# Attention by pairs of heads: 64-row logit products on both halves of the rows

## The chip, the cores and the metric

One core of one Trainium2 chip. The metric is the device time of one execution in microseconds (us). TensorE (PE) does the matrix products, VectorE (DVE), ScalarE (ACT) and GpSimd (POOL) the work on vectors, SyncE (SP) issues the transfers.

## The reference

Two layers over 1024 new frames and 32 further frames of a stream with a cache of 512, width 1024. Layer 0 mixes tokens by stick-breaking attention (16 heads of 64), layer 1 by differential attention (8 heads, each with two score maps of 64). Each mixer is followed by an output projection, a layer norm, a squared-ReLU MLP of width 4096 and another norm. Cut to what the change touches:

```python
def _stick_breaking_block(q, q_pos, k, v, k_pos):
    z = jnp.einsum('bqhd,bkhd->bhqk', q, k) * (SB_HEAD_DIM ** -0.5)
    mask = k_pos[None, :] < q_pos[:, None]
    log_keep = jnp.where(mask, jax.nn.log_sigmoid(-z), 0.0)
    after = lax.cumsum(log_keep, axis=3, reverse=True) - log_keep
    w = jnp.where(mask, jnp.exp(jax.nn.log_sigmoid(z) + after), 0.0)
    return jnp.einsum('bhqk,bkhd->bqhd', w, v)

def _diff_block(q, q_pos, k, v, k_pos, lam):
    s = jnp.einsum('bqhcd,bkhcd->bhcqk', q, k) * (DIFF_HEAD_DIM ** -0.5)
    mask = (k_pos[None, :] // CHUNK) <= (q_pos[:, None] // CHUNK)
    p = jax.nn.softmax(jnp.where(mask, s, NEG_INF), axis=-1)
    a = p[:, :, 0] - lam * p[:, :, 1]
    return jnp.einsum('bhqk,bkhe->bqhe', a, v)
```

## The kernel before

Everything is kept with features on the 128 rows and the 1056 tokens (1024 + 32, in reversed order) along the columns. A number is held as a high part and a low part in a 32-bit format, and a product is three products: high x high, high x low, low x high (lines 299 to 301, the projections and the MLP, which are most of PE's work).

A mixer (from line 981) runs two streams of work that are written into each other. One is the supply (line 1092): projection units of q, k and v, 24 tiles of 128 outputs, each over three groups of 384, 384 and 288 tokens, and after them the first seven eighths of the output projection for group 0. The other is the attention of the eight pairs of heads. `fill` (line 1154) lets as much supply run as the attention's paid columns say, so that projections stand between the steps of attention on PE. The tile scheduler then orders the instructions of each engine by what is ready and by which buffers are free.

Attention of one head goes by pairs of query blocks (128 queries each). `scores` (line 684) makes a tile of logits of up to 512 keys for one block: a block `i` takes the keys from `i` to 7, cut at 4, so that a head has 12 tiles, 6 of 512 columns and 2 each of 384, 256 and 128. q's tile holds the high part of one head in 64 rows and its low part in the other 64; k's tile holds the high part twice, and `kl` the low part over zeros:

```python
        nc.tensor.matmul(z, q[:, qs], k[:, ks], start=True, stop=False)
        nc.tensor.matmul(z, q[:, qs], kl[:, ks], start=False, stop=b0 > i)
        if b0 == i:
            nc.tensor.matmul(z[:, 0:P], self.identb, mask, start=False, stop=True)
```

So two products over all 128 rows give the three partial products of one head, and a bf16 product adds the mask on the diagonal block. In layer 0 `stick` (715) then takes two sigmoids on ACT (725, 726), a running product on DVE (727) and a product (730); in layer 1 `softmax` (858) takes a maximum (863) and an exponential (869). `flip` (733) turns the weights around on PE (745), and ACT and DVE take them out of the bank as high and low parts (748, 146). `apply` (752) multiplies them with the values (761). `head_in` (640) makes the q and k tiles out of a projection: ACT lines 654 and 655, DVE lines 656 and 657, POOL's subtraction at line 146. The 32 further frames have small products of their own (lines 704, 708, 772, 774, 837, 838, 949, 950).

The eight banks of PSUM are dealt out as three for logits (`pz`), two for transposes and small sums (`pt`), one for outputs (`px`) and two for projections (`pd`).

Of the kernel before, what the change touches and what calls it, by code (L numbers as in the profile page):

```python
# [12 lines left out]
F32 = mybir.dt.float32  # L13
# [20 lines left out]
LEADS, LEADD = 0, 24  # L34
# [8 lines left out]
AHEAD = 2, 2  # L43
# [25 lines left out]
class Trunk:  # L69
# [5 lines left out]
    def __init__(self, ctx, tc, a):  # L75
# [5 lines left out]
        self.pz = ctx.enter_context(tc.tile_pool(name="pz", bufs=3, space=PSUM))  # L81
        self.pt = ctx.enter_context(tc.tile_pool(name="pt", bufs=2, space=PSUM))
# [175 lines left out]
    @staticmethod  # L258
    def qkv_order(kind):

        if kind == "diff":
            return [t for p in range(NP) for t in (2 * p, 2 * p + 1, 2 * NP + p)]
        order = [0, 2 * NP]
        for p in range(NP):
            order += [2 * p + 1] + ([2 * NP + p + 1, 2 * p + 2] if p + 1 < NP else [])
        return order
# [120 lines left out]
    def norm_last(self, pool, y, idx, g, s, x=None, dest=None):  # L387
# [28 lines left out]
        ps = self.pt.tile([P, 2, NQ], F32, name="pc", tag="pt")  # L416
# [61 lines left out]
    def token_means(self, t, n):  # L478
# [3 lines left out]
        ps = self.pt.tile([P, NQ], F32, name="pc", tag="pt")  # L482
# [9 lines left out]
    def spread(self, r, n, exact=False):  # L492
# [4 lines left out]
        if exact:  # L497
# [3 lines left out]
            ps = self.pt.tile([P, 512], F32, name="pr", tag="pt")[:, :n]  # L501
# [6 lines left out]
        ps = self.pt.tile([P, 512], F32, name="pr", tag="pt")[:, :n]  # L508
# [131 lines left out]
    def head_in(self, kind, h, g, raw, dst):  # L640
# [4 lines left out]
        if kind == "diff":  # L645
# [14 lines left out]
        if g == NG - 1:  # L660
            j = h % 2
            js = slice(j * HD, (j + 1) * HD)
            nc.vector.tensor_scalar(qd[js, j * DEC:(j + 1) * DEC], raw[qs, n - DEC:], SCALE, None, op0=ALU.mult)
            nc.vector.tensor_copy(kd[js], raw[ks, n - DEC:])
# [19 lines left out]
    def scores(self, qk, i, b0, b1, mask):  # L684

        nc = self.nc
        q, k, kl = qk
# [27 lines left out]
    def stick(self, z, n, rows, carry):  # L715
# [17 lines left out]
    def flip(self, pair, i2, b):  # L733
# [4 lines left out]
        ps = self.pt.tile([P, 4, P], F32, name="pt", tag="pt")  # L738
# [13 lines left out]
    def apply(self, po, wt, i2, b, prods):  # L752

        order = (b + 1, b) if b == i2 else (b, b + 1)
        for kb in order:
            for e, (v, s) in enumerate(prods(kb)):
                r = wt[:, s, kb - b]
                o = po
                if kb == i2:
                    r, o = r[:, P:], po[:, :P]  # L760
                self.nc.tensor.matmul(o, v, r, start=kb == i2 + 1 and b == i2 and e == 0,  # L761
                                      stop=b == NQ - 2 and kb == order[1] and e == len(prods(kb)) - 1)
# [218 lines left out]
    def mixer(self, kind, x, res, xpool, side, grow):  # L981
# [199 lines left out]
        for m in range(ahead):  # L1181
            for f in prepare(m):
                f()
# [211 lines left out]
```

## Time and profile before

| | |
|---|---|
| Median of 3 runs | 2953.78 us (2953.05 to 2954.75) |
| Profiled execution, its own time | 2956.23 us |
| Its span from the first to the last instruction | 2954.2 us |
| PE / DVE / ACT / POOL busy | 2823.1 / 1851.4 / 1244.9 / 1055.4 us |
| Attention of layer 0, with the projections in it | about 18 to 606 us |
| Attention of layer 1, with the projections in it | about 1480 to 2070 us |

A busy PE includes the tail of each product, which runs under the next one; the distance from one start to the next tells what a product takes out of PE's time. Between the two attention stages lie the output projection, the norms and the MLP.

### The profile page before, as it was taken

The page shows a single profiled execution, that of the slowest core. Times are in us where ns is not written, and L with a number is a line of the kernel's source. Part 1 is how long each engine was busy: PE and PEld are TensorE (multiplying, and loading weights), DVE is VectorE, ACT ScalarE, POOL GpSimd, SP SyncE. Part 2 cuts the span into 40 slices and gives each one's busy share as a digit, 9 for nine tenths or more (in the row PEclk, how much of TensorE's full clock was granted, in tenths as well). Part 3 has the DMA queues.
Part 4 walks back from the last instruction along what each step waited for, and adds up shares of the span by engine and source line. Part 5 has one row for each costly group of instructions (what it writes and reads, how often), then busy time and mean ns, then how long its engine had stood idle before and what let it go on. Part 6 is the DMA issues. An engine that isn't in the chain of part 4 may idle for free.

```text
span 2954.2 us, 46333 instructions
## 1 busy us (share of the span) xinstructions
PE 2823.1 (96%) x17640; PEld 2703.3 (92%) x17640; DVE 1851.4 (63%) x3491; ACT 1244.9 (42%) x2715; POOL 1055.4 (36%) x840
## 2 busy tenths in 40 slices
PE   8999999898999999999889999998989999999997
PEld 7888888798999999999878888886989999999996
DVE  7999999969533323334878888888695333223347
ACT  6666666635222211222545555555352222212224
POOL 3222222455322222222665554554653222222233
PEclk9999999899999999999989999997999999999998
DMA  4111111252211111111421111112522111111113
GB/s 152 57 52 56 56 51 35 67 169 79 65 44 46 47 43 50 45 53 54 135 71 50 52 55 54 57 57 81 178 71 63 47 47 47 45 46 47 51 58 102
DMA packets 106622, 194.78 MB, mean 66 GB/s; under 512 B 12704, under 2 KB 30496, under 8 KB 106272
## 3 DMA queue, kind: packets, MB, share of 16 engines
q1 hardware_dynamic: 105680, 189.17, 20.8%
q8 instruction: 139, 2.28, 0.3%
q10 hardware_dynamic: 576, 1.57, 0.1%
q0 software_dynamic: 144, 1.08, 0.1%
q14 instruction: 83, 0.68, 0.1%
HBM read 159.33 MB, written 32.44 MB: 65 GB/s over the span
## 4 chain that ended last, share of the span: by engine, by line
PE 68%; DVE 22%; issue 3%; ACT 3%; POOL 2%; DMA 1%; SPq 0%; DVEq 0%; ACTq 0%; POOLq 0%
PE pd L299 20%; PE pd L300 20%; PE pd L301 20%; DVE keep L727 4%; PE po L761 2%; DVE wt L146 2%; DVE beta L730 2%; PE pt L745 2%; DVE nmax L863 1%; DVE q L657 1%; ACT e L869 1%; PE z L691 1%; DVE k L656 1%; PE z L692 1%; DVE vacc L373 1%
## 5 line engine op out<-in xcount | busy, mean ns | idle before, releaser
L299 PE MATMUL pd<-xh,w 128*128 128x384 f32 (+1 forms) x2688 | 888.1, 331 | 20.1 <-ACT xh L1233 6.3
L300 PE MATMUL pd<-xl,w 128*128 128x384 f32 (+1 forms) x2688 | 876.1, 326 | 2.4 <-DVE xl L472 1.5
L301 PE MATMUL pd<-xh,w 128*128 128x384 f32 (+1 forms) x2688 | 877.4, 327 | 0.0
L146 POOL TENSOR_TENSOR w<-wraw,w 128x512 fp32r<-128x512 f32 x306 | 419.2, 1378 | 596.7 <-ACT w L196 582.8
L299 PEld LDWEIGHTS pd<-xh,w 128*128 128x128 f32 x2688 | 510.6, 190 | 36.3 <-issue 8.9
L300 PEld LDWEIGHTS pd<-xl,w 128*128 128x128 f32 x2688 | 510.1, 190 | 9.4 <-DVE xl L472 2.6
L299 PE MATMUL pd<-h,w 128*128 128x384 f32 (+1 forms) x1536 | 501.0, 327 | 11.3 <-DVE y L588 9.7
L301 PEld LDWEIGHTS pd<-xh,w 128*128 128x128 f32 x2688 | 509.8, 190 | 1.2
L146 POOL TENSOR_TENSOR w<-arena,w 128x512 fp32r<-128x512 f32 x189 | 256.7, 1361 | 710.4 <-ACT w L196 705.2
L300 PE MATMUL pd<-h,w 128*128 128x384 f32 (+1 forms) x1536 | 501.1, 326 | 1.1 <-DVE h L146 1.1
L301 PE MATMUL pd<-h,w 128*128 128x384 f32 (+1 forms) x1536 | 499.2, 325 | 0.0
L588 DVE TENSOR_TENSOR y<-y,pd 128x384 f32<-128x384 f32 (+1 forms) x336 | 174.0, 519 | 383.6 <-PE pd L301 383.3
L574 DVE TENSOR_TENSOR arena<-arena 128x384 f32<-128x384 f32 (+1 forms) x192 | 163.6, 853 | 357.5 <-ACT arena L573 357.2
L196 ACT CAST w<-wraw 128x512 fp32r<-128x512 f32 x307 | 189.1, 619 | 409.2 <-PE pd L300 343.6
L299 PEld LDWEIGHTS pd<-h,w 128*128 128x128 f32 x1536 | 292.6, 191 | 13.4 <-issue 6.0
L300 PEld LDWEIGHTS pd<-h,w 128*128 128x128 f32 x1536 | 293.3, 191 | 2.0 <-DVE h L146 1.4
L301 PEld LDWEIGHTS pd<-h,w 128*128 128x128 f32 x1536 | 292.9, 191 | 0.1
L196 ACT CAST w<-arena 128x512 fp32r<-128x512 f32 x189 | 116.7, 620 | 356.0 <-PE pd L300 330.2
L727 DVE TENSOR_TENSOR_SCAN keep<-keep,cols 128x512 f32<-128x512 f32 (+2 forms) x208 | 220.6, 1071 | 6.4 <-ACT keep L725 4.8
L761 PE MATMUL po<-wt,vt 128*128 128x256 f32 (+1 forms) x1120 | 193.7, 296 | 6.7 <-DVE ot L346 3.9
L573 ACT ACTIVATE arena<-pd 128x384 f32<-128x384 f32 (+1 forms) x192 | 88.7, 462 | 248.2 <-PE pd L301 240.0
L146 POOL TENSOR_TENSOR kl<-arena,k 64x384 fp32r<-64x384 f32 (+1 forms) x96 | 99.0, 1032 | 226.7 <-ACT k L655 206.0
(216 smaller groups left out, 4462.7 us busy)
## 6 DMA issues: line engine op xcount, KB each, us to landing
arena<-down SPq DMA_DIRECT2D x90, 256.0 KB, 2.6
wraw<-up SPq DMA_DIRECT2D x72, 256.0 KB, 2.6
arena<-up SPq DMA_DIRECT2D x72, 256.0 KB, 2.6
wraw<-down SPq DMA_DIRECT2D x70, 256.0 KB, 2.6
wraw<-sb_o SPq DMA_DIRECT2D x48, 256.0 KB, 2.7
wraw<-diff_o SPq DMA_DIRECT2D x48, 256.0 KB, 2.7
wraw<-diff_qkv SPq DMA_DIRECT2D x45, 256.0 KB, 2.7
wraw<-sb_qkv SPq DMA_DIRECT2D x24, 256.0 KB, 3.1
```

The costliest lines, as they stand in the source:

```text
L146: eng.tensor_tensor(out, x, hi.bitcast(F32), op=ALU.subtract)
L196: nc.scalar.copy(w[:, 0], raw)
L299: self.nc.tensor.matmul(ps, wh, xh, start=first, stop=False)
L300: self.nc.tensor.matmul(ps, wh, xl, start=False, stop=False)
L301: self.nc.tensor.matmul(ps, wl, xh, start=False, stop=last)
L573: nc.scalar.activation(r, ps, AF.Relu)
L574: nc.vector.tensor_tensor(r, r, r, op=ALU.mult)
L588: nc.vector.tensor_tensor(yo, yo, ps, op=ALU.add)
L727: nc.vector.tensor_tensor_scan(keep[:rows, 1:1 + n], keep[:rows, 1:1 + n], self.zero[:rows].broadcast_to([rows, n]), keep[:rows, 0:1], op0 ...
L730: nc.vector.tensor_tensor(beta[:rows, :n], beta[:rows, :n], keep[:rows, :n], op=ALU.mult)
L745: nc.tensor.transpose(ps[:, e], w[:, (kb - wb) * P:(kb - wb + 1) * P], self.ident)
L761: self.nc.tensor.matmul(o, v, r, start=kb == i2 + 1 and b == i2 and e == 0, stop=b == NQ - 2 and kb == order[1] and e == len(prods(kb)) - 1)
```

## The change

The two heads of a pair are taken together. The projections of q and k come in tiles of 128 rows with head 0 in the upper and head 1 in the lower 64 rows (`heads`, the weights' layout), and `head_in` makes a high and a low tile of each (`qh`, `ql`, `kh`, `kl`) in one instruction for both heads. `scores` makes two tiles of logits at once, in two banks, with three products over 64 rows for each, written so that the heads alternate. The masks come after all six. Three banks for logits and two for transposes become five for both; output, weights and masks stay. In layer 0 a job is now a pair of query blocks of both heads, whose outputs share a bank; steps of preparation are dealt out one by one between the steps of `flip`; the supply leads by 24 steps in layer 0 too, and its order is q, k, v in both layers. The first column of ones of `stick` is set once in four tiles of their own.

```diff
-        self.pz = ctx.enter_context(tc.tile_pool(name="pz", bufs=3, space=PSUM))
-        self.pt = ctx.enter_context(tc.tile_pool(name="pt", bufs=2, space=PSUM))
+        self.pz = ctx.enter_context(tc.tile_pool(name="pz", bufs=5, space=PSUM))
...
-        q, k, kl, qs, ks, qd, kd = dst
-        nc.sync.dma_start(out=self.a["o_" + kind + "_k"][h, :, gs], in_=raw[ks])
-        nc.scalar.mul(q[qs, gs], raw[qs], SCALE)
-        nc.scalar.copy(k[ks, gs], raw[ks])
-        nc.vector.tensor_copy(k[qs, gs], raw[ks])
-        nc.vector.scalar_tensor_tensor(q[ks, gs], raw[qs], SCALE, q[qs, gs].bitcast(F32),
-                                       op0=ALU.mult, op1=ALU.subtract)
-        self.lo(kl[qs, gs], raw[ks], k[ks, gs], nc.gpsimd)
...
+        hi, lo, own = dst
+        if t % 2:
+            keys = self.a["o_" + kind + "_k"][t - 1:t + 1, :, gs]
+            nc.sync.dma_start(out=keys.rearrange("h d t -> (h d) t"), in_=raw)
+            nc.scalar.copy(hi[:, gs], raw)
+            self.lo(lo[:, gs], raw, hi[:, gs], nc.gpsimd)
+            if g == NG - 1:
+                nc.scalar.copy(own, raw[:, n - DEC:])
+        else:
+            nc.scalar.mul(hi[:, gs], raw, SCALE)
+            nc.vector.scalar_tensor_tensor(lo[:, gs], raw, SCALE, hi[:, gs].bitcast(F32),
+                                           op0=ALU.mult, op1=ALU.subtract)
...
     def scores(self, qk, i, b0, b1, mask):
...
-        z = self.pz.tile([P, 512], F32, name="z", tag="z")[:, :n]
-        nc.tensor.matmul(z, q[:, qs], k[:, ks], start=True, stop=False)
-        nc.tensor.matmul(z, q[:, qs], kl[:, ks], start=False, stop=b0 > i)
-        if b0 == i:
-            nc.tensor.matmul(z[:, 0:P], self.identb, mask, start=False, stop=True)
-        self.pay(self.price[0] * n)
-        return z
+        zs = [self.pz.tile([P, 512], F32, name="z", tag="z")[:, :n] for _ in range(2)]
+        for e, (q, k) in enumerate(((qh, kh), (ql, kh), (qh, kl))):
+            for j, z in enumerate(zs):
+                js = slice(j * HD, (j + 1) * HD)
+                nc.tensor.matmul(z, q[js, qs], k[js, ks], start=e == 0, stop=e == 2 and b0 > i)
+        for z in zs:
+            if b0 == i:
+                nc.tensor.matmul(z[:, 0:P], self.identb, mask, start=False, stop=True)
+            self.pay(self.price[0] * n)
+        return zs
...
-        keep = self.att.tile([P, 520], F32, name="keep", tag="keep", bufs=4)
-        beta = self.att.tile([P, 512], F32, name="beta", tag="beta", bufs=6)
         if carry is None:
-            nc.vector.memset(keep[:rows, 0:1], 1.0)
+            keep = self.whole_sticks[0]
+            self.whole_sticks.rotate(-1)
         else:
-            nc.vector.tensor_copy(keep[:rows, 0:1], carry)
+            keep = self.att.tile([P, 520], F32, name="keep", tag="keep", bufs=2)
+            nc.scalar.copy(keep[:rows, 0:1], carry)
+        beta = self.att.tile([P, 512], F32, name="beta", tag="beta", bufs=BETAS)
...
-        ps = self.pt.tile([P, 4, P], F32, name="pt", tag="pt")
+        ps = self.pz.tile([P, 4, P], F32, name="pt", tag="z")
...
-            e = self.att.tile([P, 512], F32, name="e", tag="e", bufs=8)[:rows, :z.shape[1]]
+            e = self.att.tile([P, 512], F32, name="e", tag="e", bufs=12)[:rows, :z.shape[1]]
...
-                es = [self.softmax([self.scores(st["qk"][2 * p + h], i, b0, b1, self.maskb[:, P:2 * P])
-                                    for b0, b1 in chunks], P, (s0, s1[:, 0:1])[h]) for h in range(2)]
+                zs = [self.scores(st["qk"][p], i, b0, b1, self.maskb[:, P:2 * P]) for b0, b1 in chunks]
+                es = [self.softmax([z[h] for z in zs], P, (s0, s1[:, 0:1])[h]) for h in range(2)]
...
-        nqk, nout, self.nwt = (4, 1, 3) if diff else (2, 3, 4)
-        ahead, lag, lead = AHEAD[diff], LAG[diff], LEADD if diff else LEADS
+        nout, self.nwt = (1, 3) if diff else (2, 4)
+        ahead, lag, lead = AHEAD[diff], LAG[diff], LEAD
...
-            nc.gpsimd.dma_start(out=self.rope, in_=self.a["rope"])
+            nc.sync.dma_start(out=self.rope, in_=self.a["rope"])
...
-                nc.gpsimd.memset(kl[ks].bitcast(F32), 0.0)
...
-            todo = prepare(n + ahead) if n + ahead < len(jobs) else []
+            more = len(jobs[n + 1][2]) if n + 1 < len(jobs) else 0
             for e, f in enumerate(fins):
...
+                prepare(goal + -(-more * (e + 1) // len(fins)))
                 wait.append((p, f()))
```

How it moves the instructions on PE, at two places. A name's number is that of its tile: `z_...` is a tile of logits, `q`, `k`, `kl` before and `qh`, `ql`, `kh`, `kl` after are the tiles of queries and keys, `pd` a projection, `po` the outputs, `pt` transposes.

PE at the start of layer 0's attention, before:

```order
L691 MATMUL z_438<-k_183,q_182 128x512
L691 MATMUL z_448<-k_183,q_182 128x512
L691 MATMUL z_458<-k_183,q_182 128x256
L692 MATMUL z_458<-kl_184,q_182 128x256
L694 LDWEIGHTS identb_139
L694 MATMUL z_458<-maskb_141,identb_139 128x128
L301 MATMUL pd_397<-xh_89,w_83 128x384
L299 MATMUL pd_397<-xh_89,w_83 128x384
L692 MATMUL z_438<-kl_184,q_182 128x512
L692 MATMUL z_448<-kl_184,q_182 128x512
```

The same place after:

```order
L693 MATMUL z_523<-kh_188,qh_184 128x384
L693 MATMUL z_524<-kh_188,qh_184 128x384
L693 MATMUL z_523<-kh_188,ql_185 128x384
L693 MATMUL z_524<-kh_188,ql_185 128x384
L693 MATMUL z_523<-kl_189,qh_184 128x384
L693 MATMUL z_524<-kl_189,qh_184 128x384
L696 LDWEIGHTS identb_136
L696 MATMUL z_523<-maskb_138,identb_136 128x128
L696 LDWEIGHTS identb_136
L696 MATMUL z_524<-maskb_138,identb_136 128x128
```

Two products for each tile of one head became six alternating ones for the tiles of two heads (523 and 524), and the two masks stand behind them.

PE in layer 1, at the third and fourth query block of a pair, before:

```order
L691 MATMUL z_18949<-k_17693,q_17692 128x256
L692 MATMUL z_18949<-kl_17694,q_17692 128x256
L694 LDWEIGHTS identb_139
L694 MATMUL z_18949<-maskb_141,identb_139 128x128
L691 MATMUL z_18965<-k_17343,q_17342 128x128
L692 MATMUL z_18965<-kl_17344,q_17342 128x128
L694 LDWEIGHTS identb_139
L694 MATMUL z_18965<-maskb_141,identb_139 128x128
L761 MATMUL po_18680<-wt_18911,vt_17936 128x256 x6
```

There after:

```order
L693 MATMUL z_19929<-kh_19112,qh_18758 128x512
L693 MATMUL z_19929<-kh_19112,ql_18759 128x512
L693 MATMUL z_19929<-kl_19113,qh_18758 128x512
L294 MATMUL pd_20049<-xh_7247,w_79 128x384
L693 MATMUL z_19930<-kh_19112,qh_18758 128x512
L693 MATMUL z_19930<-kh_19112,ql_18759 128x512
L693 MATMUL z_19930<-kl_19113,qh_18758 128x512
L295 MATMUL pd_20049<-xl_7248,w_79 128x384
```

Here the two heads' tiles (19929 and 19930) stand apart: three products of one head, a projection product, three of the other.

## Rows read from the trace of the kernel before

**Rows 1.** The page, busy us, share of the span, instructions, of PE.

```profile
PE 2823.1 (96%) x17640; PEld 2703.3 (92%) x17640; DVE 1851.4 (63%) x3491; ACT 1244.9 (42%) x2715; POOL 1055.4 (36%) x840
```

**Rows 2.** Stretches of the two attention stages: busy us and count by engine, clock, DMA.

```profile
core 0: us, PE busy (x) PEld busy (x) DVE busy (x) ACT busy (x) POOL busy (x), PEclk, DMA share, GB/s
18.00:606.00 588.00, 554.93 (x3705) 508.54 (x3704) 537.92 (x1036) 392.81 (x895) 162.33 (x127) 0.99 0.20 60
1480.00:2070.00 590.00, 543.16 (x3377) 484.24 (x3376) 493.03 (x1194) 332.81 (x860) 315.26 (x287) 0.95 0.20 60
```

**Rows 3.** Waits of PE in the two stages: us in total, times, longest.

```profile
PE pt L745 <- DVE wt L146: 11.2, 17, 2.4
PE pt L745 <- DVE keep L722: 7.6, 8, 1.2
PE z L691 <- DVE k L656: 7.3, 1, 7.3
...
PE z L691 <- ACT e L869: 13.3, 12, 2.4
```

**Rows 4.** Timeline of PE in layer 0: start, busy us, instruction.

```profile
299.93 0.39 PE L691 MATMUL z<-k,q 128*128 128x512 f32 x1
300.16 0.39 PE L692 MATMUL z<-kl,q 128*128 128x512 f32 x1
300.39 0.23 PE L694 MATMUL z<-maskb,identb 128*128 128x128 bf16 x1
300.43 0.42 PE L299 MATMUL pd<-xh,w 128*128 128x384 f32 x1
300.69 0.34 PE L300 MATMUL pd<-xl,w 128*128 128x384 f32 x1
...
301.04 0.34 PE L691 MATMUL z<-k,q 128*128 128x384 f32 x1
301.21 0.34 PE L692 MATMUL z<-kl,q 128*128 128x384 f32 x1
...
302.26 0.28 PE L691 MATMUL z<-k,q 128*128 128x256 f32 x1
302.38 0.28 PE L692 MATMUL z<-kl,q 128*128 128x256 f32 x1
...
303.60 0.22 PE L691 MATMUL z<-k,q 128*128 128x128 f32 x1
303.66 0.27 PE L692 MATMUL z<-kl,q 128*128 128x128 f32 x1
303.77 0.23 PE L694 MATMUL z<-maskb,identb 128*128 128x128 bf16 x1
```

**Rows 5.** Timeline of PE around products of 64 and 32 rows.

```profile
84.61 0.34 PE L301 MATMUL pd<-xh,w 128*128 128x384 f32 x1
84.87 0.23 PE L772 MATMUL pts<-ident,beta 64*32 64x64 f32 x1
...
1585.65 0.72 PE L949 MATMUL pos<-wts,cv 128*128 128x32 f32 x5
1586.21 0.48 PE L691 MATMUL z<-k,q 128*128 128x512 f32 x1
1586.53 0.40 PE L692 MATMUL z<-kl,q 128*128 128x512 f32 x1
...
1660.41 0.40 PE L950 MATMUL pos<-wts,vs 32*128 32x32 f32 x2
1660.75 0.44 PE L691 MATMUL z<-k,q 128*128 128x384 f32 x1
1661.03 0.33 PE L692 MATMUL z<-kl,q 128*128 128x384 f32 x1
```

**Rows 6.** Groups by line, DVE: count, busy us, mean ns, idle before.

```profile
L657 DVE SCALAR_TENSOR_TENSOR q<-arena,q 64x384 fp32r<-64x384 f32 (+1 forms) x96 | 67.4, 702 | 4.2 <-ACT q L654 1.2
...
L656 DVE CAST k<-arena 64x384 fp32r<-64x384 f32 (+1 forms) x96 | 51.7, 539 | 14.6 <-ACT arena L1052 11.9
...
L724 DVE COPY keep<-keep 128x1 f32<-128x1 f32 (+1 forms) x72 | 10.2, 142 | 0.0
```

More of the change, by code (lines that the diff above doesn't have):

```diff
@@ L259, in qkv_order @@
     def qkv_order(kind):
[L261 to L266, printed above, removed]
+        return [t for p in range(NP) for t in (2 * p, 2 * p + 1, 2 * NP + p)]
     def weave(self, budget, us):
@@ L760, in apply @@
                     r, o = r[:, P:], po[:, :P]
-                self.nc.tensor.matmul(o, v, r, start=kb == i2 + 1 and b == i2 and e == 0,
-                                      stop=b == NQ - 2 and kb == order[1] and e == len(prods(kb)) - 1)
+                self.nc.tensor.matmul(o, v, r, start=kb == i2 + 1 and b == i2 and e == 0 and not shared,
+                                      stop=b == NQ - 2 and kb == order[1] and e == len(prods(kb)) - 1,
+                                      skip_group_check=self.two)
                 self.pay(self.price[3])
@@ new lines, in sb_jobs, with prep, fin, later @@
+        for i2 in range(0, NQ, 2):
+            left, box = {}, []
+            for c0, c1 in (((i2, 4), (4, NQ)) if i2 < 4 else ((i2, NQ),)):
+                ws = {}
+                def prep(e, i2=i2, c0=c0, c1=c1, ws=ws, left=left):
+                    i = i2 + e
+                    b0 = max(c0, i)
+                    for j, z in enumerate(self.scores(st["qk"][p], i, b0, c1, self.maskb[:, 0:P])):
+                        w, left[i, j] = self.stick(z, (c1 - b0) * P, P, left.get((i, j)))
+                        ws[j, e] = (w, b0)
+                def fin(j, b, i2=i2, ws=ws, box=box):
+                    wt = self.flip([ws[j, 0], ws[j, 1]], i2, b)
+                    vt = st["val"][p][0]
+                    def later():
+                        if not box:
+                            box.append(self.px.tile([P, 512], F32, name="po", tag="po"))
+                        po = box[0]
+                        self.apply(po[:, j * 2 * P:(j + 1) * 2 * P], wt, i2, b, lambda kb: [
+                            (vt[:, kb, j].rearrange("p a b -> p (a b)"), s) for s in range(2)], j > 0)
+                        if b == NQ - 2 and j:
+                            t = self.att.tile([HD, 512], F32, name="vlo", tag="vlo")
+                            nc.scalar.copy(t, po[HD:P])
+                            qs = slice(i2 * P, (i2 + 2) * P)
+                            for h in range(2):
+                                hs = slice(h * 2 * P, (h + 1) * 2 * P)
+                                nc.vector.tensor_tensor(st["out"](p)[h * HD:(h + 1) * HD, qs], po[0:HD, hs],
+                                                        t[:, hs], op=ALU.add)
+                    return later
+                jobs.append((p, [lambda e=e, f=prep: f(e) for e in range(2)],
+                             [lambda j=j, b=b, f=fin: f(j, b) for j in range(2) for b in range(c0, c1, 2)]))
@@ L996, in mixer @@
         xs = self.of_groups(x)
[L997 removed]
+        st = {"qk": {}, "val": {}, "small": {}, "cache": {}, "made": {}}
         ot, spill = {}, {}
@@ L1064, in split_next @@
                 fetch["open"] = True
-                for tag in ("q", "q", "k", "k") if diff else ("kl",):
-                    backs.append(self.att.tile([P, T], F32, name="back", tag=tag, bufs=nqk if diff else 2))
+                for tag in ("qh", "ql", "kh", "kl"):
+                    backs.append(self.att.tile([P, T], F32, name="back", tag=tag, bufs=2))
             here = [k for k in ended if k not in spill and k not in whole]
@@ L1251, in run @@
                 grow()
+                self.whole_sticks = deque(self.att.tile([P, 520], F32, name="stick", tag=f"stick{i}")
+                                          for i in range(4))
+                for t in self.whole_sticks:
+                    nc.gpsimd.memset(t[:, 0:1], 1.0)
             opool, o = self.mixer(kind, x, res, xpool, sides[0], grow)
```

127 lines of the change are left out of this document (50 added, 77 removed).

## The prediction

> **What bounds the kernel now.** I read the busy table first: TensorE (PE) is busy 2823.1 us, 96% of the span [rows 1]. The table of stretches puts the change in its place: it touches the two attention stages, 18 to 606 us (stick-breaking, "sb") and 1480 to 2070 us (differential, "diff"). There PE is busy 554.9 of 588 us and 543.2 of 590 us, so 33.1 + 46.8 = 79.9 us are idle; DVE is busy 537.9 us (91%) in the first and 493.0 us (84%) in the second [rows 2]. Both stages are PE-bound, with DVE close behind in the first. So the sum below is made of PE time, and other engines count only through PE's idle time. The named waits of PE say which part of that is for whom: in sb nearly all for DVE (11.2, 7.6 and 7.3 us), in diff the longest for ACT's exponentials, which free the banks of the logits (13.3 us) [rows 3].
>
> **Part 1, the products of the logits.** On PE I read the distance from one start to the next, since the busy times overlap. Between the two products of one tile it is 0.23 us at 512 columns, 0.17 at 384, 0.12 at 256; at 128 it is 0.06 and then 0.11 [rows 4]. Before, each tile takes two 128-row products, and there are 384 tiles, 12 for each of 16 heads in two layers: by the loops 192 of 512 columns and 64 each of 384, 256 and 128. That is 192 x 0.46 + 64 x (0.35 + 0.24 + 0.17) = 137 us. After, a tile takes three 64-row products, 1152 in all. Two of them on different halves of the rows may run side by side; no row of before shows two such products next to each other. If all ran in pairs the three passes would take 576 / 2 x 0.23 + 96 x (0.17 + 0.12 + 0.11) = 105 us, 32 less than before, and that is what the change is worth at most. But the order of the changed kernel doesn't pair them all. By its tile numbers, 786 of the 1152 stand next to one of the other half; 107 runs, with 288 products and 98,944 of 442,368 columns, belong to one head alone, most of them in diff, where the second head's tile comes later (the second place shown in the order). Laid side by side where a neighbour of the other half exists and end to end elsewhere, with the distances above, they take 134 us; all end to end, 205 us. I take 134, since the halves share neither rows nor bank. **Term: -3 us** (ends -32 and +68).
> The Trainium skill ("TensorE: Matmul & The Clock Gate", Part 3, the table of measured speedups) gives 3.07 times for four 32-row tiles side by side, not 4. By that loss, an estimate of mine, two halves give 1.54 rather than 2, the paired part takes some 21 us more, and the sum below would be 2994. No row here shows it.
>
> **Part 2, the masks.** A mask product follows the tile's last product at its usual distance, the next product starts 0.04 us later, and that one then takes 0.26 rather than 0.17 us [rows 4]; so a mask costs 0.13 us, 256 of them 33 us. In the new order 94 of the 256 come directly after another mask, and such a one should cost the 0.06 us of any product of 128 columns: 94 x 0.07. **Term: -7 us** (ends -12 and 0).
>
> **Part 3, changes of the row count.** Now PE goes from 128-row products to 64-row ones and back around every run of logits: 253 runs in the new order, none before. Before, a few small products of 64 and 32 rows show what that costs [rows 5]. Into 64 rows: L301 to L772 takes 0.26 us where products of 384 columns follow each other at 0.17 [rows 4], so 0.09 more. A whole visit: the two 32-row L950 run from 1660.41 to 1660.75, 0.34 us where two L949 take 0.22 (five in 0.56 us before 1586.21), so 0.12 more, and the following L691 takes 0.28 instead of 0.17, 0.11 more. Together 0.09 + 0.12 + 0.11 = 0.32 us. But L691 behind an L949 without any change of rows also takes 0.32 instead of 0.23: 0.09 belongs to the change of type, which the new products don't have. That leaves 0.23 us a visit, and 253 x 0.23 = 58 us. 42 of the runs come directly from a mask, whose own 0.09 us is then paid anyway: -4. **Term: +54 us.** Ends: 0, if the chip prepares a 64-row product of the same type ahead as it does a 128-row one (no row shows that pair), and 253 x 0.32 = 81. A gain is excluded, as no product gets shorter by it. I take 0.23, since every row with such a change has it.
> The Trainium skill says the same of the cause ("TensorEngine Tiling (Array Packing)", Key Properties): a change of tiling mode drains the engine, a change of tile within a mode doesn't. By that rule the alternation within a run is free, and only the 253 visits are charged, as I do.
>
> **Part 4, the other engines.** head_in now works on whole 128-row tiles, once for two heads. DVE loses the copy of k (51.7 us), half of the 67.4 us for the low part of q, and small copies and memsets that go to ACT and POOL, the carry copy of 10.2 us among them [rows 6]: 51.7 + 33.7 + 10.2, some 100 us over both stages. POOL loses its memsets of the low half of k and half of the subtractions that make it. None of this is on PE's path but where PE waits for it. In sb the waits for L656 and L722 (7.3 and 7.6 us) lose their instruction, and those for DVE's subtraction behind the transposes (11.2) may halve, since DVE's load falls from 91% to some 83%: 20 us. What is late next there is the scan L727 itself, which stays. In diff I take 5 us. **Term: -25 us** (ends -50, a little over half of the 79.9 idle, and +35, the third rival).
>
> **Part 5, costed at nothing.** Attention starts one more projection tile later in sb (q, k and v of the pair must be there) and the projections lead by 24 steps: 24 x 3 x 0.17 = 12 us of products are made earlier, none is added. The partial sums of the output projection cover the end of the stage; if they don't, PE's idle time there grows by up to those 12. One more spilled tile in sb and the rotary table's load on SP's queue instead of POOL's lie under a DMA share of 0.20 [rows 2]; SP's queue then holds the weights behind one more load, once. The column of ones and the carry copies move to ACT, which is busy 392.8 of 588 us.
>
> **Sum.** -3 - 7 + 54 - 25 = +19 us. The profiled execution took 2956.23 us for a span of 2954.2; the median of the timed runs is 2953.78, and the terms are added to that: 2953.8 + 19 = **2973 us**. With the ends of the drains and idle time that this case can still have, its own range is 2948 to 3015.
>
> **The rivals.**
> *No charge for the row change.* Weights of 64-row products are loaded ahead, so entries and exits are free; the place is every one of the 253 runs. For it: all small products in [rows 5] differ from the new ones in type or width too. Against: all of them pay, in and out. Then 2954 - 3 - 7 - 25 = 2919 us, faster than before. It decides at a charge of (3 + 7 + 25) / 253 = 0.14 us a visit: below that the change wins.
> *No overlap of the halves.* The two heads' products run one after the other: 205 instead of 134 us, 2973 + 71 = 3044 us. For it: nothing in the trace shows an overlap. Against: the halves have rows, weights and banks of their own.
> *The banks become the wait.* Logits, transposes and small sums now share five banks in turn, and diff takes four at once for a block with two pieces; a transpose behind them waits until exponentials free the oldest. It happens already for 12 tiles, 1.1 us each [rows 3]. If each of the 32 such blocks paid that once, +35 us, and DVE's relief of 5 us in diff is gone: 2973 + 40 = 3013 us. Against: PE's order has projections in between.
>
> **How the numbers follow.** Forecast 0.50 (of it 0.10 within 0.2%), no charge 0.22 (0.20 faster, 0.02 within), no overlap 0.15, banks 0.13. A measurement of this kernel can tell 0.2%, some 6 us, from no change. So faster 0.20, same 0.12, slower 0.68. The range goes from 2919 to 3035: it holds the forecast, most of the first rival and the third, and leaves out the second.
>
> **What would show it.** Step 1: in the profile after, products L693 of two heads that start within a few hundredths of a us of each other, and 0.23 us per pair at 512 columns; starts 0.23 apart for each alone mean no overlap. Step 3: the first L693 after a projection product starts 0.26 rather than 0.17 us behind it, and the mask or product behind a run comes late by 0.1. Step 4: PE's idle time in the two stages down to some 55 us, DVE's busy time there down by some 100. I am wrong if the first L693 follows at 0.17, or if the two stages together end more than 10 us earlier than their 1178 us.

## The result, and the profile after

The changed kernel takes 2985.8 us in the median (2983.8 to 2986.3), the kernel before 2953.7 us beside it on the same chip: a ratio of 1.0107 with a 95% interval of 1.0090 to 1.0125. It is 32 us slower; 19 us were forecast. The sum was near, but two of its terms were not, and one cost that decides the sign is not in it at all: that the total came so near is luck.

The busy line of the page after, to be read against [rows 1]:

```profile
PE 2871.4 (96%) x18024; PEld 2700.9 (90%) x18024; DVE 1712.7 (57%) x3091; ACT 1212.3 (41%) x2739; POOL 968.8 (32%) x779
```

PE is busy 48 us longer, DVE 139 us less. The table of stretches says where; columns as in [rows 2]. These are the two attention stages and the two ends of the output projections behind them (from the last product of an attention to the last of its output projection):

```profile
33.00:626.00 593.00, 577.59 (x3886) 501.11 (x3885) 489.97 (x748) 377.30 (x936) 134.10 (x95) 0.99 0.17 59
626.00:707.00 81.00, 71.57 (x445) 70.39 (x445) 59.15 (x77) 32.51 (x52) 46.49 (x34) 0.94 0.43 139
1514.00:2081.00 567.00, 558.99 (x3528) 476.91 (x3527) 405.92 (x1052) 303.41 (x818) 260.29 (x247) 0.96 0.18 60
2081.00:2187.00 106.00, 96.16 (x575) 93.95 (x574) 71.60 (x100) 41.07 (x67) 64.18 (x47) 0.94 0.44 143
```

In attention PE now idles 15 and 8 us, where it had 33 and 38. The ends of the output projections, 72 and 92 us long before, are 81 and 106 us, and PE idles 9 and 10 us there.

To compare kernels I split each span in three. *Idle* is the time in which PE does nothing. *Clock* is what the granted clock took: for each microsecond of the trace PE's busy time times (1 - clock), added up. The rest is *work*, PE's time at its full 2.4 GHz. All in us; attention is from the first logits to the last output product, both layers; idle elsewhere includes some 6 us at the start and 8 at the end. The last two columns are the median time and its ratio to the kernel before.

| kernel | span | work | idle in attention | idle elsewhere | clock | time | ratio |
|---|---|---|---|---|---|---|---|
| before | 2954.2 | 2771.4 | 70.4 | 60.5 | 51.9 | 2953.7 | |
| after | 2984.5 | 2817.4 | 23.0 | 89.6 | 54.5 | 2985.8 | 1.0107 |
| e_norm | 2940.8 | 2823.3 | 21.8 | 62.2 | 33.5 | 2944.5 | 0.9971 |
| b_share | 2955.3 | 2768.7 | 70.6 | 63.3 | 52.7 | 2957.6 | 1.0008 |
| e_2full | 2930.0 | 2751.5 | 40.0 | 86.6 | 51.9 | 2932.8 | 0.9931 |
| e_3full | 2981.7 | 2816.2 | 33.3 | 88.0 | 44.2 | 2981.1 | 1.0094 |
| e_mid | 2996.2 | 2858.7 | 18.9 | 62.7 | 55.9 | 2997.1 | 1.0140 |
| e_noalt | 2974.6 | 2809.7 | 24.2 | 91.1 | 49.6 | 2974.0 | 1.0068 |
| e_pair01 | 2952.7 | 2801.6 | 35.4 | 65.5 | 50.2 | 2948.1 | 0.9980 |
| e_dve | 2950.3 | 2821.7 | 25.8 | 63.5 | 39.3 | 2956.4 | 1.0005 |
| e_2full4 | 2951.7 | 2760.1 | 52.2 | 89.6 | 49.8 | 2956.8 | 1.0014 |
| e_2fulldve | 2952.8 | 2756.0 | 55.4 | 91.1 | 50.3 | 2964.3 | 1.0030 |
| e_mixed | 2947.5 | 2795.1 | 48.5 | 64.8 | 39.1 | 2949.4 | 0.9986 |
| e_mixsb | 2983.3 | 2789.8 | 63.0 | 64.9 | 65.6 | 2985.1 | 1.0098 |

Each row but the time is one execution. The three kernels with the same two full products (e_2full, e_2full4, e_2fulldve) differ by 9 us in work, and some spans lie up to 12 us off their median. So differences of up to 9 us in work carry nothing, nor do those of up to some 5 us in the other columns.

From before to after: work +46, idle in attention -47, idle elsewhere +29, clock +3; together +30 of span. The prediction had +44, -25, 0, 0.

### The profile page after: what moved, and what is told of

Same layout as the page of the kernel before. It is cut to its first block, busy times and chain, and to the rows that moved or that the text cites. A ratio compares the mean times of both kernels' runs of the same rounds, so it can differ in the third digit from the quotient of the medians.

```text
span 2984.5 us, 46210 instructions
## 1 busy us (share of the span) xinstructions
PE 2871.4 (96%) x18024; PEld 2700.9 (90%) x18024; DVE 1712.7 (57%) x3091; ACT 1212.3 (41%) x2739; POOL 968.8 (32%) x779
## 4 chain that ended last, share of the span: by engine, by line
PE 81%; DVE 14%; ACT 2%; issue 1%; POOL 1%; DMA 0%; ACTq 0%; DVEq 0%; POOLq 0%
PE pd L294 23%; PE pd L295 22%; PE pd L296 22%; PE z L693 4%; PE po L765 4%; PE pt L748 2%; DVE keep L730 2%; DVE beta L733 1%; DVE stick L730 1%; ACT e L876 1%; DVE vacc L368 1%; DVE nmax L870 1%; DVE wt L146 1%; DVE xl L467 1%; PE z L696 1%
## 5 line engine op out<-in xcount | busy, mean ns | idle before, releaser
L765 PE MATMUL po<-wt,vt 128*128 128x256 f32 (+1 forms) x1120 | 182.5, 292 | 7.3 <-DVE ot L823 4.8
L765 PEld LDWEIGHTS po<-wt,vt 128*128 128x128 f32 x1120 | 156.3, 195 | 20.4 <-issue 7.8
L146 DVE TENSOR_TENSOR wt<-pt,wt 128x384 fp32r<-128x384 f32 (+1 forms) x240 | 149.5, 628 | 40.0 <-ACT wt L751 37.4
```

The source lines that it names most:

```text
L146: eng.tensor_tensor(out, x, hi.bitcast(F32), op=ALU.subtract)
```

## The experiments

### Where the time outside attention came from

The change moves the transposes' two banks into the ring of the logits. The normalizations' small tiles (`pc`, means of tokens, and `pr`, a row spread over the partitions) lay in those two banks, and they moved along, also outside attention, where the output projection and the MLP use the ring. e_norm gives them two banks of their own there:

```diff
+    def small_bank(self, shape, name):
+        pool, tag = (self.pd, "pd") if self.banks[0][0] is self.pz else (self.pz, "z")
+        return pool.tile(shape, F32, name=name, tag=tag)
...
-        ps = self.pz.tile([P, NQ], F32, name="pc", tag="z")
+        ps = self.small_bank([P, NQ], "pc")
```

(and so for the other three; the products outside attention keep the ring of five for themselves). b_share tries the reverse on the kernel before: products outside attention go round all five banks, two of them the normalizations':

```diff
-[(self.pz, "z")]
+[(self.pz, "z")] * 3 + [(self.pt, "pt")] * 2
```

> The changed kernel with one part of it undone: outside the attention stages the small tiles of a normalization (means of tokens, and the row spread over the partitions) lie in two banks of their own again (those that feed the projections' products during attention), not in the ring of five that the output projection and the MLP use for their products. Theory A, the shared ring makes TensorE wait at the normalizations' small products: its idle time outside the attention stages falls from 83 us towards the 54 us of the kernel before, and the time from 2986 to 2957 to 2972. Rival B, those waits come from the new order of the work (what is left of the output projection, the state of the weights' loads), not from the banks: 2980 to 2990.

> The kernel before with one thing of the change alone: outside the attention stages the products of the output projection and the MLP go round five banks, of which two are those of the normalizations' small tiles, as in the changed kernel (before: three banks of their own, and two for the normalizations). Attention is untouched. Theory A, it is this sharing that costs: TensorE's idle time outside attention grows by 15 to 30 us and its clock falls there too, 2970 to 2995 us. Rival B, sharing costs only with the changed kernel's other order: 2948 to 2960.

e_norm takes 2944.5 us (2942.6 to 2946.7), 0.9971 of before, interval 0.9959 to 0.9983: 41 us less than the changed kernel, more than theory A gave, and faster than before. The waits of PE over the whole span (us in total, times, longest) show what the ring did. After:

```profile
PE pc L482 <- DVE vacc L370: 41.5, 6, 7.9
PE pr L509 <- DVE diag L506: 11.8, 7, 2.7
```

The same two in e_norm, four lines further down in the file:

```profile
PE pr L513 <- DVE diag L510: 8.0, 7, 3.9
PE pc L486 <- DVE vacc L374: 7.3, 5, 2.6
```

The second of them before:

```profile
PE pc L487 <- DVE vacc L375: 9.6, 5, 2.7
```

41.5 us of waiting for the sum of squares fell to 7.3. All idle time ahead of a `pc` outside attention, whatever ended it, is 11 us before, 47 after and 22 in e_norm, so not all of it is won back. The timeline (start, busy us, instruction, and in brackets the idle time ahead) shows one of the six, in the output projection of layer 0. After:

```profile
677.09 0.29 PE L296 MATMUL pd<-oh,w 128*128 128x288 f32 x1
677.22 0.81 PE L358 MATMUL pm<-acc,onesr 128*128 128x384 f32 x2
684.80 0.37 PE L482 MATMUL pc<-onesr,vacc 128*128 128x1 f32 x1 [6.77 <-DVE vacc L370]
```

e_norm:

```profile
677.28 0.81 PE L362 MATMUL pm<-acc,onesr 128*128 128x384 f32 x2
677.63 0.59 PE L296 MATMUL pd<-oh,w 128*128 128x288 f32 x1
...
685.73 0.29 PE L295 MATMUL pd<-ol,w 128*128 128x288 f32 x1
685.87 0.50 PE L486 MATMUL pc<-onesr,vacc 128*128 128x1 f32 x4
```

Between `pm` (the mean goes out to DVE) and `pc` (the squares come back) DVE needs some 8 us. In e_norm 60 projection products fill them. In the changed kernel none stand there: `pc` comes next in PE's order, and PE waits 6.77 us. All six waits are of this kind: at these places, three in each layer, the changed kernel has 0, 33 and 63 projection products between `pm` and `pc`; e_norm, as the kernel before, has 60 at the first, 87 at the second and 101 or more at the third. So the loss is one of order: with the tiles in one ring the scheduler put the small product ahead of projections. Why it did so, no run shows.

b_share takes 2957.6 us, 1.0008 (0.9999 to 1.0017): no cost, rival B. There the ends of the output projections get longer by 6 and 7 us, but the MLP's first product comes only 2 and 3 us later, and idle time outside attention grows by 3 us in all. At the three places it has 60, 87 and over 120 products ahead of `pc`, as before. So products in the normalizations' banks don't hurt by themselves; what hurts is the place that `pc` got in the changed kernel. Of e_norm's gain 29 us is idle time and 21 us clock, against 6 us more work. 12 of the 21 are in the differential stage, where the edit leaves all tiles where they were; why the clock is better there I did not settle (last section).

### What a row change costs

Three kernels with other products. e_2full and e_3full make two or three 128-row products of each tile (no row change, no overlap), with sums that mix the heads:

```diff
+        for z in zs:
+            for e, (q, k) in enumerate(((qh, kh), (ql, kh), (qh, kl))[:2]):
+                nc.tensor.matmul(z, q[:, qs], k[:, ks], start=e == 0, stop=e == 1 and b0 > i)
```

e_mid, on e_norm, adds visits: the masks go behind the first two of the six products.

```diff
+            if e == 0 and b0 == i:
+                for z in zs:
+                    nc.tensor.matmul(z[:, 0:P], self.identb, mask, start=False, stop=False)
         for z in zs:
-            if b0 == i:
-                nc.tensor.matmul(z[:, 0:P], self.identb, mask, start=False, stop=True)
```

> The changed kernel with two 128-row products for each tile of logits in place of three 64-row ones (it sums the rows of both heads and leaves the third product out, so its logits are other numbers). No product uses half of the rows any more, so nothing overlaps and TensorE never goes from one row count to the other; the columns are those of the kernel before (294,912). Theory A, each visit to the 64-row products costs 0.30 to 0.40 us, 88 us in all, and the products themselves cost as before: TensorE's work in the two attention stages falls by 45 to 65 us, some of it comes back as idle time, and the kernel takes 2930 to 2966 us, of which the waits outside the attention stages stay. Rival B, entering and leaving costs no more than 0.23 us a visit and the rest of the growth is in the products (overlap less than full): a fall of 20 us at most, 2966 to 2986.

> The changed kernel with its three products for each tile of logits over all 128 rows (the logits of both heads are summed, so they are other numbers). The number, the sizes and nearly the places of the products stay, but there is no row change and no overlap. By the order of the instructions the products' streaming grows from 131 us to 200 us (442,368 columns at 2.207 a nanosecond), +69. Theory A (88 us for the row changes in the changed kernel): -88 + 69 = -19, with the waits that this moves 2950 to 2985. Rival B (0.23 us a visit, 54 us): +15, 2990 to 3010. Rival C (no charge for the row change at all): +69, 3040 to 3060.

> The changed kernel with the small tiles in banks of their own (2944 us, 254 visits to the 64-row products) and the mask products moved: after the first two of the six products of a pair instead of at the end. It computes the same; by the order of its instructions 401 visits in place of 254, and 126 us of streaming in place of 132. Theory A, a visit costs 0.27 us, as the kernels with 128-row products gave it: +40 - 6, and 2965 to 2985 us. Rival B, the 0.35 us by the gaps in the trace: +51 - 6, 2985 to 2995. Rival C, 0.14 us or less: 2960 at most.

Against the changed kernel e_2full loses 65.9 us of work for 3 us more streaming (134 for 131), so its 253 visits are worth 69 us. e_3full loses 1 us for 69 us more streaming, so 70. Both give 0.27 to 0.28 us a visit. Both times lie in theory A's ranges, though it had a visit at 0.30 us or more. e_mid adds 35.4 us of work with 147 visits more and 6 us less streaming: 0.28 us, theory A. By the 9 us that work varies by, e_2full and e_3full can be off by 0.04 us and e_mid by 0.06. Its time, 2997 us, is above A and B, since the clock took another 22 us. In its timeline one sees a visit that is left and entered again:

```profile
100.06 0.50 PE L697 MATMUL z<-kh,qh 64*128 64x512 f32 x2
100.49 0.28 PE L700 MATMUL z<-maskb,identb 128*128 128x128 bf16 x2
100.71 0.49 PE L697 MATMUL z<-kh,ql 64*128 64x512 f32 x2
101.05 0.40 PE L697 MATMUL z<-kl,qh 64*128 64x512 f32 x2
101.37 0.33 PE L753 MATMUL pt<-ident,beta 128*128 128x128 f32 x1
```

A pair of 512 columns streams for 0.23 us. From the first pair to the masks it takes 0.43: 0.1 for the first pair of a visit and 0.1 for leaving. The two masks take 0.22, of which 0.12 is the way back in (in the changed kernel two masks ahead of a projection product take 0.10). From the second pair to the third it is 0.34, the first pair's 0.1 once more; the last one leaves at 0.32.

### Whether the halves overlap, and what order they need

e_noalt writes three products of one head, then three of the other. e_pair01, on e_norm, pins each of the six behind the one before it on PE, so that one head can't run ahead alone:

```diff
-        for e, (q, k) in enumerate(((qh, kh), (ql, kh), (qh, kl))):
-            for j, z in enumerate(zs):
+        for j, z in enumerate(zs):
+            for e, (q, k) in enumerate(((qh, kh), (ql, kh), (qh, kl))):
```

```diff
+                if not first:
+                    self.tc.keep_in_program_order(mm)
+                first = False
```

> The changed kernel with the six products of a pair written as three of one head and then three of the other, not alternating. It computes the same. By the order of the instructions 245 visits (253 before this edit), and two of the six products then stand beside one of the other half: streaming alone 317 thousand columns against 134 thousand, 172 us against 131 us if only neighbours in the order overlap. Theory A, overlap of neighbours is what the alternation buys and TensorE is the bound: +25 to +41, 3010 to 3027. Rival B, the overlap is worth little because the reading of the logits sets the pace: 2980 to 2995.

> The changed kernel with the small tiles in banks of their own (2944 us), and an order for the six products of a pair: each stays behind the one before it on TensorE, so that the first head's three can't run ahead alone. It computes the same. By the order of its instructions 250 visits (254), and the columns that run alone fall from 139 to 41 thousand: 110 us of streaming in place of 132. Theory A, the halves overlap fully and TensorE is the bound: -22 us of work, of which up to 10 come back as idle time since the pair now waits for two banks: 2922 to 2936. Rival B, overlap is partial, or the wait for the second bank eats it: 2938 to 2950.

The changed kernel, where heads alternate, and where one is alone:

```profile
49.69 0.40 PE L693 MATMUL z<-kl,qh 64*128 64x512 f32 x2
49.93 0.39 PE L693 MATMUL z<-kh,qh 64*128 64x512 f32 x1
50.16 0.38 PE L693 MATMUL z<-kh,ql 64*128 64x512 f32 x1
...
90.84 0.34 PE L296 MATMUL pd<-xh,w 128*128 128x384 f32 x1
91.11 0.51 PE L693 MATMUL z<-kh,qh 64*128 64x512 f32 x2
91.44 0.41 PE L693 MATMUL z<-kh,ql 64*128 64x512 f32 x2
91.67 0.41 PE L693 MATMUL z<-kl,qh 64*128 64x512 f32 x2
92.01 0.44 PE L294 MATMUL pd<-xh,w 128*128 128x384 f32 x1
```

A pair takes the 0.23 us of a single product: full overlap. The Trainium skill's 3.07 times for four tiles ("TensorE: Matmul & The Clock Gate", Part 3) would make it 1.54 for two (the prediction's estimate); here it is 2. The place in e_noalt, where three products of one tile stand ahead of three of the other in the order of the instructions:

```profile
91.00 0.34 PE L296 MATMUL pd<-xh,w 128*128 128x384 f32 x1
91.27 0.51 PE L693 MATMUL z<-kh,qh 64*128 64x512 f32 x2
91.60 0.41 PE L693 MATMUL z<-kh,ql 64*128 64x512 f32 x2
91.83 0.41 PE L693 MATMUL z<-kl,qh 64*128 64x512 f32 x2
```

They start in pairs all the same. Over the runs of six with 512 columns the first and the last product start 573 ns apart in the changed kernel (median of 72) and 579 ns in e_noalt (of 76). In 149 of e_noalt's 245 visits the products start in another order than the one they stand in; the visits themselves, and all products between them, follow in the written order. So the alternation buys nothing, and my theory A for e_noalt fell: it counted neighbours in the order as the only ones that overlap. Work is 8 us less, not 41 more. The time, 2974 us, is below rival B's range too, whose reason, an overlap worth little, fell with A. Of the 10 us that the span is shorter 8 are work, which is within what work varies by, and 5 are clock: 12 less in the differential stage, some 7 more elsewhere. The Trainium skill ("TensorEngine Tiling (Array Packing)", Key Properties) says that tiles operate independently; the trace agrees.

This changes the count above. If a visit streams as long as the longer of its two halves, the changed kernel streams for 124 us in place of 131, e_noalt for 120, and e_norm and e_mid for 125 and 126. A visit is then worth 0.30 us by e_2full and e_3full and 0.24 by e_mid. This is an estimate; 0.24 to 0.30 us is what the three kernels can say.

e_pair01 loses 21.7 us of work, as overlap asks (22 by neighbours, 15 by the longer half), and takes 2948.1 us (2945.4 to 2954.5), 3.6 more than e_norm: rival B. Idle time in attention goes from 22 to 35 us and the clock's share from 33 to 50. The profiled execution was the slowest of its runs, but the others gain nothing on e_norm either. PE's waits in it, in stick-breaking and then in the differential stage:

```profile
PE pt L756 <- DVE wt L146: 6.0, 4, 2.6
PE pc L486 <- ACT e L884: 4.5, 1, 4.5
```

The same in e_norm:

```profile
PE pt L752 <- DVE wt L146: 0.6, 2, 0.4
PE pc L486 <- ACT e L880: 2.7, 1, 2.7
```

The waits of the pair itself, ahead of `z`, did not grow (7 us in e_norm, 6 here), so it isn't the second bank. What grew are waits behind the pair: for transposes from 3 to 9 us and for small rows (`pr`) from 0.5 to 5.

### What gave PE's idle time in attention back

e_dve, on e_norm, puts DVE work back that the change removed: two 64-row copies for each piece of k (and, in the branch of q, one 64-row subtraction), into a tile that nobody reads. It gives DVE 49 us back in the two stages. e_2fulldve is the same on e_2full, 59 us there; the change had taken 115 away. e_2full4 is e_2full with four banks in the ring.

```diff
+            more = self.att.tile([P, GM], BF16, name="more", tag="more")[:, :n]
+            for j in range(2):
+                js = slice(j * HD, (j + 1) * HD)
+                nc.vector.tensor_copy(more[js], raw[js])
```

```diff
-name="pz", bufs=5
+name="pz", bufs=4
```

> The changed kernel with the small tiles in banks of their own (2944 us, TensorE idle for 22 us in the two attention stages), and with DVE work put back that the change took away: two copies of 64 rows for each piece of k and one subtraction of 64 rows for each piece of q, into a tile that nobody reads, 144 instructions or some 80 us. Theory A, it was DVE's relief that took TensorE's idle time in attention from 70 us to 22: it goes back up by 20 to 45, 2962 to 2990. Rival B, the five banks in one ring and the work by pairs did it: +8 at most, 2942 to 2952.

> The kernel with two 128-row products for each tile of logits (2933 us, TensorE idle for 40 us in the two attention stages where the kernel before has 70 with as many columns; its logits sum both heads and leave the third product out, so they are other numbers), with four banks in the ring in place of five. Theory A, it was the ring of five, in place of three and two, that gave TensorE back 30 us of idle time: 15 to 30 us of idle return, 2945 to 2965 us. Rival B, it was not the banks: 2928 to 2940.

> The kernel with two 128-row products for each tile of logits (2933 us, TensorE idle for 40 us in attention; its logits sum both heads and leave the third product out), with 144 DVE instructions put back that the change took away (the copies of 64 rows of k and the subtraction of 64 rows of q, into a tile that nobody reads). With less TensorE work than in the kernel of the same kind tried before, idle time isn't hidden under it. Theory A, DVE's relief gave TensorE the 30 us back: 15 to 30 us of idle return, 2945 to 2965 us. Rival B, it was the banks or the work by pairs: 2928 to 2941.

e_dve: idle time in attention 21.8 to 25.8 us only. That is rival B's. Its time, 2956.4 us, is 12 above e_norm and in neither range; in the profile most of the rise is in the clock of the differential stage (19 us for 10), so the time doesn't tell. e_2full has 20 us less of PE's work than the kernel before, so nothing hides there: 40.0 us idle against 70.4. With four banks it is 52.2, short of theory A's 15 us of return; with DVE's work back 55.4, as theory A has it, nearly all in the differential stage (13 to 29 us). So of the 47 us, some 15 come back with half of DVE's relief taken away, and some 12 with the fifth bank; whether the ring of five gave as much against the two and three banks of before, no run shows. The other 17 lie between e_2full and the changed kernel (40.0 to 23.0). Longer PE work that covers the waits is not all of it: e_3full has as much work as the changed kernel and idles 33.3 us. So some 7 of the 17 go with the work, and 10 with the 64-row products themselves; why stays open. The times rise by 24 and 31 us, more than this idle time, and both lie in theory A's ranges. The profiled execution of e_2fulldve is the fastest of its nine, 10 us below their median, so its profile doesn't show all of the rise.

### Whether less PE work would now pay

e_mixed, on e_norm, makes the differential stage's logits as before (one head's tiles, two 128-row products), e_mixsb those of stick-breaking, where the space allows only three tiles in turn. Both put DVE's copies back with them, 57 and 63 us of DVE in the stage, and take buffers away (one tile of exponentials; two of `beta`):

```diff
+        if len(qk) == 2:
+            for z, (q, k, kl) in zip(zs, qk):
+                nc.tensor.matmul(z, q[:, qs], k[:, ks], start=True, stop=False)
+                nc.tensor.matmul(z, q[:, qs], kl[:, ks], start=False, stop=b0 > i)
```

> The changed kernel with the small tiles in banks of their own (2944 us), and in the differential stage the logits made as in the kernel before: tiles of one head with q's two halves under each other and k twice, two 128-row products for each tile, jobs still by pairs of heads. Stick-breaking keeps the 64-row products. It computes the same. About half of the row changes are gone (0.27 us each, some 125) and the streaming of diff's logits stays about the same: 30 to 36 us less work of TensorE. Theory A, the row changes are plain TensorE time: with 5 to 15 us back as idle time 2915 to 2930 us. Rival B, DVE's copies and the extra tiles (one bank more held, less room for the exponentials) take it back: 2935 to 2955.

> The mirror of the last mixed kernel, from the same base (2944 us): stick-breaking makes its logits as the kernel before does (tiles of one head, two 128-row products for each tile of logits, jobs still by pairs), with three tiles each of q, k and kl in turn and seven beta tiles, for which there is room; the differential stage keeps the 64-row products, since its time was set by ACT's exponentials as soon as TensorE had less to do. It computes the same. Some 127 row changes go, 30 to 36 us of TensorE's work. Theory A, stick-breaking is the stage where TensorE sets the time: it ends 15 to 30 us earlier, 2915 to 2932 us. Rival B, there too the time is given back, to DVE (its copies are back, 490 to some 515 us busy in a stage of 593) and to the third tile: 2938 to 2960.

Work falls by 28 and 34 us, about as expected; the time does not: 2949.4 and 2985.1 us for 2944.5. The first is rival B, the second is slower than either theory had it. PE's waits in e_mixed's differential stage:

```profile
PE z L710 <- ACT e L900: 10.2, 16, 2.2
PE pr L513 <- DVE s L928: 5.8, 4, 1.5
PE zs L734 <- ACT e L900: 3.7, 5, 2.4
```

and in e_mixsb's stick-breaking:

```profile
PE z L711 <- DVE q L658: 19.2, 7, 3.2
PE z L711 <- ACT beta L754: 15.7, 7, 2.5
```

In the differential stage the logits wait for banks that ACT's exponentials free, in stick-breaking for tiles of q that DVE makes. Since both edits also load DVE and take buffers, they don't show what less PE work alone would bring. e_2full does: the row changes, 69 us of PE's work, cost less in time. Without any of them it is 53 us faster than the changed kernel, and 17 us come back as idle time in attention.

The fastest of these that computes the reference is e_norm, 0.9971 of before.

## Why the prediction came out as it did

**Products, -3.** Right in the overlap: halves overlap fully, single runs stand 0.23 us apart. The streaming by the order is 131 us (134 by the distances in [rows 4]). That only neighbours in the order overlap was wrong, as e_noalt shows; by the longer half of each visit it is 124 us. The rival without overlap falls: it would have meant 71 us more work.

**Masks, -7.** Mask and follower cost 28 us before and 25 after: right in sign, 3 in place of 7.

**Row changes, +54.** Measured 69 us (up to 75 if the halves run on by themselves), in the range of 0 to 81. The mechanism was right, the size was not. The step that failed is the subtraction of 0.09 as a "change of type" that the new products don't have. But the extra is there with one type throughout: L693 starts 0.27 us behind a projection product of 384 columns (90.84 to 91.11) where 0.17 is usual, the second pair comes at 0.33 in place of 0.23, and leaving takes 0.1 more. Nor is the entry from a mask free: from a mask to the first L693 it is 0.15 us, to a projection product 0.03 (medians of 39 and 66). Without the subtraction the same rows [rows 5] gave 0.32 us a visit, with it 0.23; the runs gave 0.24 to 0.30. The rival without a charge needed less than 0.14 us.

**The sum of PE's work, +44.** Measured +46, but by luck: +15 in the row changes stands against some 20 us less elsewhere, where 7 were forecast. e_2full shows these: with as many columns in the products as before, its work is 20 us less. 3 of them are masks; the rest is spread over many pairs of neighbours, and I did not locate it.

**Idle time in attention, -25.** Measured -47. DVE's relief was the reason given; half of it is worth some 15. The step left out the fifth bank (some 12 us in e_2full), and PE's added work, which hides waits (some 7 of the 17 us between e_2full and the changed kernel). 10 us stay open. The 22 us more that came back nearly cancel the 29 us of the next step, and so the sum came out near.

**Costed at nothing.** This is the step that failed outright. It lists the later start, the lead, a spilled tile and the rotary table, but not that `pc` and `pr` change their pool in every normalization outside attention. +29 us of idle time and most of e_norm's 41 us are there.

**The banks as a rival** had the right resource, five banks for everything, and the wrong place: it counted transposes behind exponentials in the differential stage. There PE waits for ACT's exponentials less than before (4.6 us with a `z` or `pc` behind them, for 13.3 in [rows 3]).

**What would show it.** The pairs, the 0.27 and the 0.1 are there as named. PE's idle time in attention fell to 23, not 55; DVE's busy time between the first logits and the last output product fell by 115 in both stages, near the 100. The two stages together stayed at 1160 us, cut alike.

## What to carry to other kernels

When an edit moves a buffer to another pool, list every place that uses it, in stages the edit is not about too, and look at PE's order there: a small product that waits for another engine needs work ahead of it, and its bank decides where it stands. In a kernel like this one, price a row-count change at 0.24 to 0.30 us a visit, and count visits, not products. Split a result into work, idle time and clock before believing a sum: work saved on an engine that covers another one's time comes back as waiting. Of 22 us saved in e_pair01 14 came back as idle time in attention and 17 were lost in clock. For the 28 and 34 us of e_mixed and e_mixsb it was 27 and 41 us of idle time, DVE's copies and the missing buffers included.

## What the runs showed of the hardware

The two halves of the rows run on by themselves: six products in the order three and three started in pairs (579 ns against 573), and in 149 of e_noalt's 245 visits the start order is not the written one.

Idle time can come with a lower clock. Stretches of stick-breaking in e_norm and e_mixsb, columns as in [rows 2]:

```profile
33.00:626.00 593.00, 577.71 (x3885) 501.42 (x3884) 489.97 (x748) 376.71 (x937) 132.94 (x95) 0.99 0.18 59
```

```profile
32.00:665.00 633.00, 576.70 (x3695) 531.75 (x3693) 553.25 (x851) 394.19 (x957) 162.97 (x124) 0.93 0.18 56
```

With 41 us more idle time in many short waits, the granted clock is 0.93 in place of 0.99, and that took another 31 us: PE is busy as long as in e_norm for 34 us less work. Idle time alone doesn't set it: the kernel before idles 33 us in this stage at 0.99 [rows 2].

At the end of the differential stage the changed kernel has this stretch, 6 us of it and then 24 us at half the clock (1.2 GHz) while PE is nearly always busy:

```profile
2031.00:2034.00 3.00, 3.00 (x9) 2.06 (x9) 2.59 (x6) 1.92 (x5) 2.04 (x2) 0.50 0.00 0
2034.00:2037.00 3.00, 3.00 (x13) 2.55 (x13) 1.78 (x4) 0.00 (x0) 2.46 (x3) 0.56 0.25 87
2037.00:2040.00 3.00, 3.00 (x19) 2.20 (x18) 2.18 (x10) 1.24 (x4) 0.54 (x1) 1.00 0.24 87
2040.00:2043.00 3.00, 2.89 (x16) 1.90 (x15) 1.70 (x8) 1.31 (x5) 0.00 (x0) 1.00 0.00 0
2043.00:2067.00 24.00, 23.57 (x83) 17.60 (x84) 14.26 (x44) 11.26 (x31) 3.48 (x4) 0.51 0.01 1
```

e_norm's last 30 us of that stage:

```profile
2024.00:2054.00 30.00, 29.36 (x187) 22.43 (x188) 24.34 (x74) 19.76 (x55) 7.05 (x7) 0.94 0.11 38
```

Just ahead of the second fall, at 2043 us, PE waited 0.5 us; ahead of the first it had waited 3.2 and 0.7 us, from 2025 on. The 6.77 us of waiting in the output projection shown above were followed by a loss of 2.2 us in all of that stretch. In the kernels here the clock took 7 to 27 us of this stage, and no run was made to tell why; 12 of e_norm's 41 us hang on it.
